# First feed-forward product of a hybrid decoder layer: high weights against both halves of an activation in one 512-column product, and the halves' sums by adding DMA

## The chip, the cores and the metric

The kernel runs on one core of one Trainium2 chip. The metric is device time in microseconds; lower is better. A core has TensorE (matrix products, "PE"; its weight loads are listed as "PEld"), VectorE ("DVE"), ScalarE ("ACT"), GpSimd ("POOL") and SyncE ("SP"). DMAs are issued from the queues of SP, ScalarE and GpSimd; those that add to their destination are issued from GpSimd's queue here.

## The reference

One decoder layer on 512 tokens and 2048 features, in float32. The change lies in the feed-forward part:

```
def conv_ffn(h, w_up, conv_w, conv_b, w_down):
    u, g = jnp.split(h @ w_up, 2, axis=-1)            # w_up: 2048 x 11264, u and g: 512 x 5632
    u = lax.conv_general_dilated(u, conv_w[:, None, :], ...) + conv_b   # causal, width 3, per channel
    return (jax.nn.silu(u) * g) @ w_down

...
h = rms_norm(x, norm_ffn[l]) * (1.0 + sc2) + sh2
x = x + g2 * conv_ffn(h, w_up[l], conv_w[l], conv_b[l], w_down[l])
```

Ahead of it stand a modulation (`c_act @ w_mod`), a combined input projection, two kinds of attention and an output projection; behind it `h @ w_down` and a last RMSNorm.

## The kernel before

**Precision by halves.** Every float32 factor is split into a high half (rounded to the float32r type by ScalarE) and a low half (the rest, by VectorE's subtraction); `split_to` (L214) and `cut` (L1028) do this. A product of two such factors is three matmuls: high weight by high activation, high weight by low activation, low weight by high activation.

**The first feed-forward product.** The 5632 channels are 44 tiles `f` of 128. The first three (`NP = 3`) are done plainly, each matmul 128 weights wide and 512 tokens long. The other 41 use a factored scheme with seven products instead of eight (Winograd's form of Strassen's): the 2048 features are halved, the 512 tokens are halved (`W = 256`), and the two outputs of a tile, u and g, are the halves of the third direction. `Duo` (L1109) is one of the seven products of a tile, in the order `ORDER = (1, 2, 6, 5, 7, 3, 4)`. Its `mm` runs 8 steps over the 128-feature pieces of a half, three matmuls of 256 columns per step, into one of three PSUM banks: x holds products 1, 6, 7 and 4, z holds 2, y holds 5 and 3. Products share a bank and go on adding to it, so between two products in one bank the running value is copied or added out (`Duo.out`, L1143): product 1's value and then product 6's out of x by a ScalarE copy (L1148, L1152), product 7's by a VectorE addition (L1157), and so on. The banks hold 512 columns; 256 are used.

**Operands.** `form[i]` holds the activation side of product i as (high, low) tiles. Forms 1, 2, 3 and 5 are blocks of the normed activations, kept in eight tiles `h2h0..3` and `h2l0..3` (L1596); forms 6, 7 and 4 are sums of blocks, made by `t_forms` (L1170); form 5 is written by `t1_form` (L1188) once the plain units have read what lay there. The weight side of a tile comes as four raw pieces of 128 x 1024 (512 KB), a and b for u, c and d for g. `duo_load` (L1067) fetches them through SP, `duo_cut` (L1078) makes the seven weight combinations: a is cut first, then b, then s = d - (a - c), then c + d, then a - c, b - s and d. A piece is fetched again for tile f + 2 once its last cut is made; even tiles lie in the pool `raw2`, odd ones in `fr`, so each piece has two buffers. A cut goes into one of four weight buffers, so cuts run up to three products ahead of TensorE.

**After the products.** In `out` for product 3 the kernel starts `conv` (L1035): ScalarE applies bias and one tap (L1036), VectorE the two other taps (L1037, L1038), ScalarE SiLU (L1039). For product 4, VectorE multiplies the first 256 columns by g straight out of bank x and the others by g in store (L1164, L1165), and ScalarE issues the store to DRAM.

**Order.** A program in the kernel writes down slots (one product each). `drive` (L374) issues the weight cuts of the slots up to three ahead, then a slot's matmuls, then one `step` of every generator that runs beside them (`start` adds one, with a delay in steps). What is written first has priority; a scheduler then gives each engine a fixed order of its instructions, in which one that it holds to be ready may go ahead of one written before it. On the chip each engine works its own list in that order. Beside the products, `mod_gen` (L260) works off the last modulation columns: GpSimd's queue loads 128 x 512 pieces (`raw_mod`, L1531, four buffers), VectorE multiplies and adds them (L231), 64 pieces in the stage, paced by the number of columns that TensorE was given.

Of the kernel before, what the change touches and what calls it, by code (L numbers as in the profile page):

```python
# [8 lines left out]
F32 = mybir.dt.float32  # L9
F32R = mybir.dt.float32r  # L10
AF = mybir.ActivationFunctionType
OP = mybir.AluOpType
# [3 lines left out]
P = 128  # L16
T = 512
# [16 lines left out]
def hybrid_trunk(ctx, tc, xT, cT, wm, bm, nrm, wik, wiq, wi1, sinks, kvn, wuk, wuv, rel, onehot,  # L34
# [4 lines left out]
    class Counted:  # L39

        def __init__(self, to):
            self.to, self.cols = to, 0
# [171 lines left out]
    def split_to(hi_t, lo_t, full, keep=False):  # L214
        hi = act.copy(hi_t, full)  # L215
        if keep:
            tc.keep_in_program_order(hi)
        dve.tensor_tensor(lo_t, full, hi_t.bitcast(F32), OP.subtract)  # L218
# [86 lines left out]
    def pace(gen, every):  # L305
        paced.append([gen, every, pe.cols])
# [650 lines left out]
    slots = []  # L957
# [47 lines left out]

    class Rows:

        def __init__(self, tiles):
            self.t = tiles

        def __getitem__(self, key):
            return self.t[key[1] // 4][:, :, key[1] % 4]

    acts, ugate = {}, {}
    x2d = [dram.tile([P, 4, T], F32, name=f"x2d{i}") for i in range(4)]
# [12 lines left out]
    def cut(x, name):  # L1028

        w = env["px0"].tile([P, 2, 1024], F32R, tag=f"x2_{cut_turn[0] % 4}", name=f"w{name}")  # L1030
        cut_turn[0] += 1
        split_to(w[:, 0], w[:, 1], x)
        return w[:, 0], w[:, 1]

    def conv(f, y, u):  # L1035
        act.activation(y, u, AF.Identity, bias=cb_sb[:, f:f + 1], scale=cw_sb[:, f, 2:3])  # L1036
        dve.scalar_tensor_tensor(y[:, 1:], u[:, :T - 1], cw_sb[:, f, 1:2], y[:, 1:], OP.mult, OP.add)  # L1037
        dve.scalar_tensor_tensor(y[:, 2:], u[:, :T - 2], cw_sb[:, f, 0:1], y[:, 2:], OP.mult, OP.add)  # L1038
        act.activation(y, y, AF.Silu)  # L1039
# [24 lines left out]

    duo_raw = {}

    def duo_load(f, tag):  # L1067
        if f >= FT:
            return
        row, half = {"a": (0, 0), "b": (0, 1), "c": (1, 0), "d": (1, 1)}[tag]  # L1070
        if f % 2:
            t = fr_tile(tag, f"r{tag}{f}")
        else:
            t = env["raw2"].tile([P, 1024], F32, tag=tag, name=f"r{tag}{f}")
        duo_raw[f, tag] = t
        sp.dma_start(t, wup[2 * f + row].rearrange("p a b -> p (a b)")[:, 1024 * half:1024 * half + 1024])

    def duo_cut(f, pos):  # L1078
        a, b, c, d = [duo_raw[f, t] for t in "abcd"]
        name = f"u{f}_{pos}"  # L1080
        if pos == 0:
            return cut(a, name)
        if pos == 1:
            w = cut(b, name)
            dve.tensor_tensor(a, a, c, OP.subtract)
            return w
        if pos == 2:
            s = duo_raw[f, "s"] = fr_tile("s", f"rs{f}")
            dve.tensor_tensor(s, d, a, OP.subtract)  # L1089
            return cut(s, name)  # L1090
        if pos == 3:
            dve.tensor_tensor(c, c, d, OP.add)
            w = cut(c, name)
            duo_load(f + 2, "c")
            return w
        if pos == 4:
            w = cut(a, name)
            duo_load(f + 2, "a")
            return w
        if pos == 5:  # L1100
            dve.tensor_tensor(b, b, duo_raw[f, "s"], OP.subtract)
            w = cut(b, name)
            duo_load(f + 2, "b")
            return w
        w = cut(d, name)
        duo_load(f + 2, "d")
        return w

    class Duo:  # L1109
# [11 lines left out]
        def mm(self, w):  # L1121
            box, i = self.box, ORDER[self.pos]
            if i == 1:
                box["x"] = bank("acc", f"ux{self.f}")[:, :W]
            elif i == 2:
                box["z"] = bank("sc", f"uz{self.f}")[:, :W]
            elif i == 5:
                box["y"] = bank("tp", f"uy{self.f}")[:, :W]
            ps = box[{2: "z", 5: "y", 3: "y"}.get(i, "x")]
            new = i in (1, 2, 5)  # L1130
            ah, al = form[i]
            go = {} if new else {"skip_group_check": True}
            for k in range(8):
                wh, wl = [x[:, P * k:P * k + P] for x in w]
                xh, xl = [x[k // 4][:, k % 4] for x in (ah, al)]
                pe.matmul(ps, wh, xh, start=new and k == 0, stop=False, **go)
                pe.matmul(ps, wh, xl, start=False, stop=False, **go)
                pe.matmul(ps, wl, xh, start=False, stop=k == 7, **go)

        def after(self):  # L1140
            start(self.out())
# [1 line left out]
        def out(self):  # L1143
            f, box, i = self.f, self.box, ORDER[self.pos]
            ut = env["ut"]
            if i == 1:
                box["u"] = ut.tile([P, T], F32, tag="u", bufs=2, name=f"ut{f}")
                act.copy(box["u"][:, :W], box["x"])  # L1148
            elif i == 2:
                dve.tensor_tensor(box["u"][:, :W], box["u"][:, :W], box["z"], OP.add)  # L1150
            elif i == 6:
                act.copy(box["u"][:, W:], box["x"])  # L1152
            elif i == 5:
                box["g"] = ut.tile([P, W], F32, tag="g", bufs=2, name=f"gt{f}")
                act.copy(box["g"], box["y"])
            elif i == 7:
                dve.tensor_tensor(box["g"], box["g"], box["x"], OP.add)  # L1157
            elif i == 3:
                dve.tensor_tensor(box["u"][:, W:], box["u"][:, W:], box["y"], OP.add)
                box["o"] = ut.tile([P, T], F32, tag="y", bufs=3, name=f"y{f}")  # L1160
                conv(f, box["o"], box["u"])
            else:
                y = box["o"]
                dve.tensor_tensor(y[:, :W], box["x"], y[:, :W], OP.mult)  # L1164
                dve.tensor_tensor(y[:, W:], box["g"], y[:, W:], OP.mult)  # L1165
                yield
                store_act(f, y)
            yield

    def t_forms():  # L1170

        x2, tt = env["x2"], env["tt"]
        h, l = [x.t for x in env["h2"]]
        for i, j, tok in ((1, 0, 0), (2, 2, 0), (3, 2, 1), (5, 0, 1)):
            form[i] = [[x[j + q][:, tok] for q in range(2)] for x in (h, l)]
        for i in (6, 7, 4):
            t = tt.tile([P, 2, 8, W], F32R, tag=f"t{i}", name=f"t{i}_up")
            form[i] = [[t[:, x, 4 * q:4 * q + 4] for q in range(2)] for x in range(2)]
        for j in range(2):
            q11, q12, q21, q22 = [x2[k][:, :, c:c + W] for k in (j, j + 2) for c in (0, W)]  # L1180
            for i, q, x, y, op in ((7, q22, q22, q12, OP.subtract), (None, q12, q12, q11, OP.subtract),
                                   (6, q11, q11, q22, OP.add), (4, q21, q21, q11, OP.subtract)):
                dve.tensor_tensor(q, x, y, op)
                if i:
                    split_to(form[i][0][j], form[i][1][j], q)
                    yield

    def t1_form():  # L1188
        for j in range(2):
            split_to(form[5][0][j], form[5][1][j], env["x2"][j][:, :, W:])  # L1190


    down_t = {}
# [335 lines left out]
        return two[0][:, kt % 2]  # L1529

    def raw_mod(g, kt):  # L1531
        t = env["ut"].tile([P, 512], F32, tag="mr", bufs=4, name=f"mraw{g}_{kt}")
        pool.dma_start(t, wm[g, kt // 4][:, kt % 4])  # L1533
        return t

# [57 lines left out]
    for dt in range(0, KT, 4):  # L1593
        dve.scalar_tensor_tensor(a2[:, dt:dt + 4], mod[:, 16 + dt // 4], 1.0, nrm_sb[:, 1, dt:dt + 4],
                                 OP.add, OP.mult)
    form_t = [[big.tile([P, 2, 4, W], F32R, tag=f"b{'hl'[i]}{j}", name=f"h2{'hl'[i]}{j}") for j in range(4)]  # L1596
              for i in range(2)]
    env["h2"] = [Rows(x) for x in form_t]
    halves = lambda x: x.rearrange("p (a b) -> p a b", a=2)
    for i in range(4):  # L1600
        for kt in range(4 * i, 4 * i + 4):
# [13 lines left out]
    ringc.__exit__(None, None, None)  # L1615
    rawc = tc.tile_pool(name="raw2", bufs=1, side="right", reuse_waits="tile")
    env["raw2"] = rawc.__enter__()
    for t in "abcd":
        duo_load(NP + 1, t)
    utc = tc.tile_pool(name="ut", bufs=1, side="right", reuse_waits="tile")  # L1620
    env["ut"] = utc.__enter__()
    pace(mod_gen(range(20, 24), raw_mod, 3, env["ut"], o_bank), 28000)
    drive(slots, marks["duo"], marks["down"] - 7, ahead=3)
    down_t["stage0"] = {}
    for k in range(2):
        for c in range(2):
            t = env["raw2"].tile([P, 1024], F32, tag="abcd"[2 * k + c], name=f"stage0_{k}{c}")
            down_t["stage0"][k, c] = t = t.rearrange("p (a b) -> p a b", a=4)
            sp.dma_start(t, actd[k][:, :, W * c:W * c + W])
    drive(slots, marks["down"] - 7, marks["down"] - 3, ahead=3)  # L1630
    down_tiles()
    for t in "acdb":
        for p in range(2):
# [122 lines left out]
```

## Time and profile before

| | before |
|---|---|
| median of 3 runs | 2130.55 us (2129.72 to 2136.72) |
| the profiled execution | 2132.93 us, of which its span is 2131.1 us |
| granted TensorE clock, mean | 0.994 |
| TensorE, VectorE, ScalarE, GpSimd busy | 98%, 81%, 54%, 8% of the span |
| stage of the factored products (827.8 to 1662 us) | 834.2 us, 6934 matmuls |

A profile's page lists busy time and shares of the span by engine. A grouped row has the line in the kernel, engine, operation, output <- inputs, shapes and count, then busy time, mean ns of one, and the idle time before them with what ended it. A row of the timeline has start, duration, engine, line, operation, tiles and count. Matmuls are pipelined, so the mean duration of one (283 ns for 256 columns) is longer than the distance from one to the next. Instructions on VectorE overlap a little too.

### The profile page before, as it was taken

The page shows a single profiled execution, that of the slowest core. Times are in us where ns is not written, and L with a number is a line of the kernel's source. Part 1 is how long each engine was busy: PE and PEld are TensorE (multiplying, and loading weights), DVE is VectorE, ACT ScalarE, POOL GpSimd, SP SyncE. Part 2 cuts the span into 40 slices and gives each one's busy share as a digit, 9 for nine tenths or more (in the row PEclk, how much of TensorE's full clock was granted, in tenths as well). Part 3 has the DMA queues.
Part 4 walks back from the last instruction along what each step waited for, and adds up shares of the span by engine and source line. Part 5 has one row for each costly group of instructions (what it writes and reads, how often), then busy time and mean ns, then how long its engine had stood idle before and what let it go on. Part 6 is the DMA issues. An engine that isn't in the chain of part 4 may idle for free.

```text
span 2131.1 us, 34497 instructions
## 1 busy us (share of the span) xinstructions
PE 2080.6 (98%) x13346; PEld 1832.2 (86%) x13346; DVE 1716.1 (81%) x2522; ACT 1143.2 (54%) x1907; POOL 180.4 (8%) x310
## 2 busy tenths in 40 slices
PE   8999999999999999999999999999999999999997
PEld 4777877777788889999999999999999787787787
DVE  2887899877868788888788888888887987787867
ACT  4324887777722274444444444444444575675654
POOL 0000000111033200000000000000000011111110
PEclk9999999999999999999999999999999999999998
DMA  9773122666699724444444435435344888898982
GB/s 390 272 289 111 55 72 60 186 212 215 192 374 319 241 83 141 157 134 134 148 116 158 140 118 159 137 126 159 122 132 126 282 248 216 228 235 209 217 232 83
DMA packets 125029, 385.18 MB, mean 181 GB/s; under 512 B 14783, under 2 KB 24015, under 8 KB 118080
## 3 DMA queue, kind: packets, MB, share of 16 engines
q1 hardware_dynamic: 84096, 257.16, 36.8%
q0 software_dynamic: 31264, 108.51, 19.3%
q10 hardware_dynamic: 9504, 17.31, 2.2%
q8 instruction: 104, 1.70, 0.3%
q14 instruction: 61, 0.50, 0.1%
HBM read 324.46 MB, written 58.46 MB: 180 GB/s over the span
## 4 chain that ended last, share of the span: by engine, by line
PE 80%; DVE 8%; DMA 5%; ACT 4%; issue 3%; POOL 0%; SPq 0%; DVEq 0%; POOLq 0%; ACTq 0%
PE ux L53 21%; PE p L53 14%; PE uy L53 11%; PE uz L53 5%; PE qip L53 4%; DMA qa<-in_wdn_dram 1%; DMA mraw<-in_wm_dram 1%; PE ckv L53 1%; PE mrow L53 1%; DVE wd L218 1%; PE o L53 1%; DVE wk L688 1%; DMA rawca<-in_wdn_dram 1%; DVE top L685 1%; PE mps L53 1%
## 5 line engine op out<-in xcount | busy, mean ns | idle before, releaser
L53 PE MATMUL p<-wd,af 128*128 128x512 f32 x1680 | 386.3, 391 | 12.4 <-DVE wd L218 9.6
L53 PEld LDWEIGHTS p<-wd,af 128*128 128x128 f32 x1680 | 315.5, 188 | 82.8 <-DVE wd L218 13.7
L53 PE MATMUL ux<-t_up,wu 128*128 128x256 f32 x2952 | 375.3, 283 | 0.0
L53 PEld LDWEIGHTS ux<-t_up,wu 128*128 128x128 f32 x2952 | 362.9, 192 | 0.9 <-DVE gt L1157 0.2
L53 PE MATMUL uy<-h2h,wu 128*128 128x256 f32 x1312 | 249.6, 283 | 0.0
L53 PEld LDWEIGHTS uy<-h2h,wu 128*128 128x128 f32 x1312 | 210.6, 192 | 0.0
L231 DVE SCALAR_TENSOR_TENSOR macc<-mraw,c_sb,macc 128x512 f32<-128x512 f32 x240 | 179.5, 748 | 9.8 <-DMA mraw<-in_wm_dram 7.8
L53 PE MATMUL uy<-h2l,wu 128*128 128x256 f32 x656 | 185.6, 283 | 0.0
L218 DVE TENSOR_TENSOR wu<-ra,wu 128x1024 fp32r<-128x1024 f32 x82 | 100.2, 1222 | 63.0 <-ACT wu L215 63.0
L215 ACT CAST wu<-rb 128x1024 fp32r<-128x1024 f32 x82 | 86.0, 1048 | 111.3 <-PE ux L53 63.3
L215 ACT CAST wu<-ra 128x1024 fp32r<-128x1024 f32 x82 | 85.7, 1045 | 100.6 <-PE uy L53 60.9
L53 PEld LDWEIGHTS uy<-h2l,wu 128*128 128x128 f32 x656 | 125.9, 192 | 0.0
L53 PE MATMUL uz<-h2h,wu 128*128 128x256 f32 x656 | 124.8, 283 | 0.0
L53 PE MATMUL ux<-h2h,wu 128*128 128x256 f32 x656 | 124.8, 283 | 0.0
L218 DVE TENSOR_TENSOR wu<-rb,wu 128x1024 fp32r<-128x1024 f32 x82 | 100.1, 1220 | 8.4 <-ACT wu L215 8.4
L53 PEld LDWEIGHTS ux<-h2h,wu 128*128 128x128 f32 x656 | 105.3, 192 | 0.0
L53 PEld LDWEIGHTS uz<-h2h,wu 128*128 128x128 f32 x656 | 105.3, 192 | 0.0
L1533 POOL DMA_DIRECT2D mraw<-in_wm_dram x64 | 34.3, 536 | 797.7 <-DVE macc L231 621.8
L218 DVE TENSOR_TENSOR wu<-rd,wu 128x1024 fp32r<-128x1024 f32 x41 | 50.2, 1225 | 63.8 <-ACT wu L215 63.8
L1344 ACT COPY ev<-p 128x512 f32<-128x512 f32 x140 | 81.5, 583 | 26.0 <-PE p L53 18.7
L215 ACT CAST wu<-rs 128x1024 fp32r<-128x1024 f32 x41 | 43.2, 1053 | 95.3 <-DVE rs L1089 53.3
L53 PE MATMUL ux<-h2l,wu 128*128 128x256 f32 x328 | 92.8, 283 | 0.0
(1739 smaller groups left out, 4792.9 us busy)
## 6 DMA issues: line engine op xcount, KB each, us to landing
mraw<-in_wm_dram POOLq DMA_DIRECT2D x160, 256.0 KB, 5.4
total<-ev POOLq DMA_DIRECT2D x70, 512.0 KB, 8.0
mraw<-in_wm_dram SPq DMA_DIRECT2D x32, 1024.0 KB
mraw<-in_wm_dram POOLq DMA_DIRECT2D x48, 512.0 KB, 6.6
ra<-in_wup_dram SPq DMA_DIRECT2D x41, 512.0 KB
rc<-in_wup_dram SPq DMA_DIRECT2D x41, 512.0 KB
rb<-in_wup_dram SPq DMA_DIRECT2D x41, 512.0 KB
rd<-in_wup_dram SPq DMA_DIRECT2D x41, 512.0 KB
```

The source lines that it names most:

```text
L53: return self.to.matmul(out, w, x, **kw)
L215: hi = act.copy(hi_t, full)
L218: dve.tensor_tensor(lo_t, full, hi_t.bitcast(F32), OP.subtract)
L231: tc.keep_in_program_order(dve.scalar_tensor_tensor(acc, t, cact[:, kt:kt + 1], acc, OP.mult, OP.add))
L685: dve.max(top[b][:, r], cur[b])
L688: dve.match_replace(wk[b], top[b][:, r], cur[b], -3e38)
L1344: act.copy(e[:, b], ps)
L1533: pool.dma_start(t, wm[g, kt // 4][:, kt % 4])
```

## The change

In the factored products:

- The step of three matmuls of 256 columns becomes two: the high weight meets high and low activation side by side, as one matmul of 512 columns, and the low weight meets the high activation in one of 256. The bank then holds two sums side by side, which have to be added: [:, 0] has high by high and low by high, [:, 1] has high by low.
- So the copies and additions out of PSUM are 512 columns wide (256 tokens, both sums). The two sums of u and of g's second half are added by a DMA on GpSimd's queue that adds one part of a tile to the other in SBUF; g's first half is copied by ScalarE and its second sum added by VectorE. `conv` starts two steps after product 4's output and reads the summed u; one multiply of 512 columns replaces two of 256.
- c + d is no longer made by VectorE for tiles past the first factored one: SP loads c a second time, into a tile e, and a DMA on GpSimd's queue adds d from DRAM to it. c has one buffer (in `fr`), and so has e (in `raw2`); both are fetched again one tile ahead instead of two.
- The normed activations lie in eight tiles of [high/low, token half, two pieces], so that both halves of a piece can be one operand; the forms change with them, and form 5 is made by four splits instead of two.
- Tiles: u is [2, 512] and g [3, 256] with two buffers each, y has two buffers instead of three, mod's raw pieces two instead of four (loaded one ahead instead of two). At the end of the stage the four first loads of the next stage go out one slot later, one of them into e's place.

```
 class Rows:
-    def __init__(self, tiles):
-        self.t = tiles
+    def __init__(self, tiles, part):
+        self.t, self.part = tiles, part
     def __getitem__(self, key):
-        return self.t[key[1] // 4][:, :, key[1] % 4]
+        return self.t[key[1] // 2][:, self.part, :, key[1] % 2]
...
+def duo_part(f, tag):
+    row, half = {"a": (0, 0), "b": (0, 1), "c": (1, 0), "d": (1, 1)}[tag]
+    return wup[2 * f + row].rearrange("p a b -> p (a b)")[:, 1024 * half:1024 * half + 1024]
+
+def duo_sum(f):
+    pool.dma_start(duo_raw[f, "e"], duo_part(f, "d"), accum_op=OP.add)
+    yield
+
 def duo_load(f, tag):
     if f >= FT:
         return
-    row, half = {"a": (0, 0), "b": (0, 1), "c": (1, 0), "d": (1, 1)}[tag]
-    if f % 2:
+    if f % 2 and tag != "e" or tag == "c":
         t = fr_tile(tag, f"r{tag}{f}")
     else:
         t = env["raw2"].tile([P, 1024], F32, tag=tag, name=f"r{tag}{f}")
     duo_raw[f, tag] = t
-    sp.dma_start(t, wup[2 * f + row].rearrange("p a b -> p (a b)")[:, 1024 * half:1024 * half + 1024])
+    sp.dma_start(t, duo_part(f, "c" if tag == "e" else tag))
+    if tag == "e":
+        start(duo_sum(f), 2)
...
     if pos == 1:
         w = cut(b, name)
         dve.tensor_tensor(a, a, c, OP.subtract)
+        if f > NP:
+            duo_load(f + 1, "c")
         return w
...
     if pos == 3:
-        dve.tensor_tensor(c, c, d, OP.add)
-        w = cut(c, name)
-        duo_load(f + 2, "c")
+        if f > NP:
+            w = cut(duo_raw[f, "e"], name)
+            duo_load(f + 1, "e")
+        else:
+            dve.tensor_tensor(c, c, d, OP.add)
+            w = cut(c, name)
+            duo_load(f + 1, "c")
         return w
...
 def mm(self, w):
-        box["x"] = bank("acc", f"ux{self.f}")[:, :W]
+        box["x"] = bank("acc", f"ux{self.f}", (P, 2, W))
...
-    ah, al = form[i]
...
         wh, wl = [x[:, P * k:P * k + P] for x in w]
-        xh, xl = [x[k // 4][:, k % 4] for x in (ah, al)]
-        pe.matmul(ps, wh, xh, start=new and k == 0, stop=False, **go)
-        pe.matmul(ps, wh, xl, start=False, stop=False, **go)
-        pe.matmul(ps, wl, xh, start=False, stop=k == 7, **go)
+        x = form[i][k]
+        pe.matmul(ps, wh, x, start=new and k == 0, stop=False, **go)
+        pe.matmul(ps[:, 0], wl, x[:, 0], start=False, stop=k == 7, **go)
...
 def out(self):
     if i == 1:
-        box["u"] = ut.tile([P, T], F32, tag="u", bufs=2, name=f"ut{f}")
-        act.copy(box["u"][:, :W], box["x"])
+        box["u"] = ut.tile([P, 2, T], F32, tag="u", bufs=2, name=f"ut{f}")
+        act.copy(box["u"][:, :, :W], box["x"])
     elif i == 2:
-        dve.tensor_tensor(box["u"][:, :W], box["u"][:, :W], box["z"], OP.add)
+        dve.tensor_tensor(box["u"][:, :, :W], box["u"][:, :, :W], box["z"], OP.add)
     elif i == 6:
-        act.copy(box["u"][:, W:], box["x"])
+        act.copy(box["u"][:, :, W:], box["x"])
     elif i == 5:
-        box["g"] = ut.tile([P, W], F32, tag="g", bufs=2, name=f"gt{f}")
-        act.copy(box["g"], box["y"])
+        box["g"] = ut.tile([P, 3, W], F32, tag="g", bufs=2, name=f"gt{f}")
+        act.copy(box["g"][:, 1:], box["y"])
     elif i == 7:
-        dve.tensor_tensor(box["g"], box["g"], box["x"], OP.add)
+        g = box["g"]
+        dve.tensor_tensor(g[:, 1:], g[:, 1:], box["x"], OP.add)
+        pool.dma_start(g[:, 1], g[:, 2], accum_op=OP.add)
     elif i == 3:
-        dve.tensor_tensor(box["u"][:, W:], box["u"][:, W:], box["y"], OP.add)
-        box["o"] = ut.tile([P, T], F32, tag="y", bufs=3, name=f"y{f}")
-        conv(f, box["o"], box["u"])
+        u = box["u"]
+        dve.tensor_tensor(u[:, :, W:], u[:, :, W:], box["y"], OP.add)
+        pool.dma_start(u[:, 0], u[:, 1], accum_op=OP.add)
     else:
-        y = box["o"]
-        dve.tensor_tensor(y[:, :W], box["x"], y[:, :W], OP.mult)
-        dve.tensor_tensor(y[:, W:], box["g"], y[:, W:], OP.mult)
+        g, x = box["g"], box["x"]
+        act.copy(g[:, 0], x[:, 0])
+        dve.tensor_tensor(g[:, 0], g[:, 0], x[:, 1], OP.add)
+        for _ in range(2):
+            yield
+        y = ut.tile([P, T], F32, tag="y", bufs=2, name=f"y{f}")
+        conv(f, y, box["u"][:, 0])
+        dve.tensor_tensor(y, y, g[:, 0:2].rearrange("p a b -> p (a b)"), OP.mult)
         yield
         store_act(f, y)
...
 def t1_form():
-    for j in range(2):
-        split_to(form[5][0][j], form[5][1][j], env["x2"][j][:, :, W:])
+    for q in range(4):
+        t = env["fq"][q]
+        split_to(t[:, 0, 1], t[:, 1, 1], env["x2"][q // 2][:, 2 * (q % 2):2 * (q % 2) + 2, W:])
...
-    t = env["ut"].tile([P, 512], F32, tag="mr", bufs=4, name=f"mraw{g}_{kt}")
+    t = env["ut"].tile([P, 512], F32, tag="mr", bufs=2, name=f"mraw{g}_{kt}")
...
-for t in "abcd":
+for t in "abde":
     duo_load(NP + 1, t)
...
-pace(mod_gen(range(20, 24), raw_mod, 3, env["ut"], o_bank), 28000)
-drive(slots, marks["duo"], marks["down"] - 7, ahead=3)
+pace(mod_gen(range(20, 24), raw_mod, 2, env["ut"], o_bank), 28000)
+drive(slots, marks["duo"], marks["down"] - 6, ahead=3)
```

More of the change, by code (lines that the diff above doesn't have):

```diff
@@ L1123, in mm @@
             if i == 1:
-                box["x"] = bank("acc", f"ux{self.f}")[:, :W]
+                box["x"] = bank("acc", f"ux{self.f}", (P, 2, W))
             elif i == 2:
-                box["z"] = bank("sc", f"uz{self.f}")[:, :W]
+                box["z"] = bank("sc", f"uz{self.f}", (P, 2, W))
             elif i == 5:
-                box["y"] = bank("tp", f"uy{self.f}")[:, :W]
+                box["y"] = bank("tp", f"uy{self.f}", (P, 2, W))
             ps = box[{2: "z", 5: "y", 3: "y"}.get(i, "x")]
             new = i in (1, 2, 5)
-            ah, al = form[i]
             go = {} if new else {"skip_group_check": True}
@@ L1172, in t_forms @@
         x2, tt = env["x2"], env["tt"]
-        h, l = [x.t for x in env["h2"]]
-        for i, j, tok in ((1, 0, 0), (2, 2, 0), (3, 2, 1), (5, 0, 1)):
-            form[i] = [[x[j + q][:, tok] for q in range(2)] for x in (h, l)]
+        for i, k0, tok in ((1, 0, 0), (2, 8, 0), (3, 8, 1), (5, 0, 1)):
+            form[i] = [env["fq"][(k0 + k) // 2][:, :, tok, k % 2] for k in range(8)]
+        made = {}
         for i in (6, 7, 4):
-            t = tt.tile([P, 2, 8, W], F32R, tag=f"t{i}", name=f"t{i}_up")
-            form[i] = [[t[:, x, 4 * q:4 * q + 4] for q in range(2)] for x in range(2)]
+            t = made[i] = tt.tile([P, 2, 8, W], F32R, tag=f"t{i}", name=f"t{i}_up")
+            form[i] = [t[:, :, k] for k in range(8)]
         for j in range(2):
@@ L1184, in t_forms @@
                 if i:
-                    split_to(form[i][0][j], form[i][1][j], q)
+                    split_to(*[made[i][:, x, 4 * j:4 * j + 4] for x in range(2)], q)
                     yield
     def t1_form():
-        for j in range(2):
-            split_to(form[5][0][j], form[5][1][j], env["x2"][j][:, :, W:])
+        for q in range(4):
+            t = env["fq"][q]
+            split_to(t[:, 0, 1], t[:, 1, 1], env["x2"][q // 2][:, 2 * (q % 2):2 * (q % 2) + 2, W:])
     down_t = {}
@@ L1595, in hybrid_trunk @@
                                  OP.add, OP.mult)
-    form_t = [[big.tile([P, 2, 4, W], F32R, tag=f"b{'hl'[i]}{j}", name=f"h2{'hl'[i]}{j}") for j in range(4)]
-              for i in range(2)]
-    env["h2"] = [Rows(x) for x in form_t]
+    env["fq"] = [big.tile([P, 2, 2, 2, W], F32R, tag=f"b{'hl'[q % 2]}{q // 2}", name=f"h2_{q}") for q in range(8)]
+    env["h2"] = [Rows(env["fq"], i) for i in range(2)]
     halves = lambda x: x.rearrange("p (a b) -> p a b", a=2)
@@ L1626, in hybrid_trunk @@
         for c in range(2):
-            t = env["raw2"].tile([P, 1024], F32, tag="abcd"[2 * k + c], name=f"stage0_{k}{c}")
+            t = env["raw2"].tile([P, 1024], F32, tag="abed"[2 * k + c], name=f"stage0_{k}{c}")
             down_t["stage0"][k, c] = t = t.rearrange("p (a b) -> p a b", a=4)
             sp.dma_start(t, actd[k][:, :, W * c:W * c + W])
-    drive(slots, marks["down"] - 7, marks["down"] - 3, ahead=3)
+    drive(slots, marks["down"] - 6, marks["down"] - 3, ahead=3)
     down_tiles()
```

## Prediction

> **What bounds the kernel now.** I read the page first, then the table of stretches for the stage that the change touches, then the order of instructions inside it, and last the landing times of DMAs. The page gives the shares of the span:
>
> ```profile
> span 2131.1 us, 34497 instructions
> ...
> PE 2080.6 (98%) x13346; PEld 1832.2 (86%) x13346; DVE 1716.1 (81%) x2522; ACT 1143.2 (54%) x1907; POOL 180.4 (8%) x310
> ```
>
> TensorE is busy for 98% of the span, so a change pays only if TensorE gets less to do, or costs if it is made to wait. The stretch from the first factored product to the last (827.8 to 1662 us) is even tighter:
>
> ```profile
> core 0: us, PE busy (x) PEld busy (x) DVE busy (x) ACT busy (x) POOL busy (x), PEclk, DMA share, GB/s
> 827.80:1662.00 834.20, 834.20 (x6934) 832.79 (x6933) 690.38 (x805) 388.43 (x495) 33.25 (x62) 1.00 0.45 143
> ```
>
> TensorE has no gap here and the granted clock is 1.00. VectorE fills 83% and ScalarE 47%, GpSimd (the queue that issues adding DMAs) 4%, the DMA engines 45%. There are 41 units of 7 products, 56 steps of three matmuls each, so 6888 of the 6934 matmuls are the subject of the change, and one unit takes 834.2/41 = 20.35 us (20.2 without the other 46 matmuls).
>
> **The products.** What counts is the spacing of matmuls, not the mean duration of one, since they overlap. First narrow ones (256 columns) of a factored product, then wide ones (512 columns) of the plain products just before the stage:
>
> ```profile
> 999.81 0.28 PE L53 MATMUL uy<-h2l,wu 128*128 128x256 f32 x1
> ...
> 1000.17 0.28 PE L53 MATMUL uy<-h2l,wu 128*128 128x256 f32 x1
> ...
> 1000.53 0.28 PE L53 MATMUL uy<-h2l,wu 128*128 128x256 f32 x1
> ```
>
> ```profile
> 790.11 0.39 PE L53 MATMUL g0ps<-h2l,g0r_3h 128*128 128x512 f32 x1
> ...
> 792.84 0.39 PE L53 MATMUL u1ps<-h2l,u1r_3h 128*128 128x512 f32 x1
> ```
>
> The h2l matmul comes back every 0.36 us with two others between, so a narrow one takes 120.0 ns. Between the two wide rows lie 12 spacings: 2.73/12 = 227.5 ns. A step is now 3 x 120.0 = 360.0 ns and becomes 227.5 + 120.0 = 347.5 ns. It saves 12.5 ns, 0.70 us per unit, and over 41 x 56 = 2296 steps **28.7 us**. A unit goes from 20.2 to 19.5 us, a product from 2.88 to 2.78 us. Weight loads fall from three to two per step; the narrow spacing already holds one load each, so nothing is added there. The wide plain products read an operand made of two strided halves too, so the form [2, 256] has a row.
>
> The Trainium skill speaks against this gain: "TensorE: Matmul & The Clock Gate", section "Back-to-back issue gap", gives N/2.4 + 2.5 ns, so 109 ns at 256 columns, and an estimate by it is 2.5 ns saved per step, 5.7 us in all. The trace differs (120.0 ns measured at a granted clock of 1.00), and I take the trace.
>
> **VectorE and ScalarE.** Rows of the grouped view, with shapes kept apart:
>
> ```profile
> L1092 DVE TENSOR_TENSOR rc<-rc,rd 128x1024 f32<-128x1024 f32 x41 | 50.0, 1219 | 0.0
> ...
> L543 DVE TENSOR_TENSOR qi<-qi,qip 128x512 f32<-128x512 f32 x56 | 38.3, 684 | 14.4 <-PE qip L53 13.7
> ...
> L1344 ACT COPY ev<-p 128x512 f32<-128x512 f32 x140 | 81.5, 583 | 26.0 <-PE p L53 18.7 <-DMA total<-ev 7.3
> ...
> L1036 ACT ACTIVATE y<-ut,cb_sb,cw_sb 128x512 f32<-128x512 f32 x41 | 33.4, 815 | 1.6 <-DVE ut L1159 1.6
> ...
> L1165 DVE TENSOR_TENSOR y<-gt,y 128x256 f32<-128x256 f32 x41 | 17.0, 416 | 0.0
> ...
> L1157 DVE TENSOR_TENSOR gt<-gt,ux 128x256 f32<-128x256 f32 x41 | 17.0, 414 | 0.2 <-PE ux L53 0.2
> ...
> L1152 ACT COPY ut<-ux 128x256 f32<-128x256 f32 x41 | 15.0, 366 | 0.0
> ```
>
> VectorE loses c + d (1.22 us, now an adding DMA). The three additions out of PSUM grow from 256 to 512 columns: 3 x (0.684 - 0.414) = 0.81 us. A fourth addition (0.41) is new, and two multiplies of 0.416 become one of at most 0.684. Sum: -1.22 + 0.81 + 0.41 - 0.15 = -0.15 us per unit. From 690.4/41 = 16.8 us it goes to 16.7, which is 86% of 19.5: still not the bound. ScalarE gains 3 x (0.583 - 0.366) + 0.37 = 1.0 us on 9.5, 54%. Both are hidden on the whole; the question is where a copy or addition out of PSUM gates the next product in the same bank.
>
> The order inside a unit shows how much room there is: VectorE's addition L1157, which must end before the next product into the same bank begins, then TensorE's and ScalarE's rows at the same places:
>
> ```profile
> 925.68 0.41 DVE L1157 TENSOR_TENSOR gt<-gt,ux 128x256 f32<-128x256 f32 x1
> ...
> 1005.35 1.22 DVE L218 TENSOR_TENSOR wu<-rb,wu 128x1024 fp32r<-128x1024 f32 x1
> 1006.48 0.41 DVE L1157 TENSOR_TENSOR gt<-gt,ux 128x256 f32<-128x256 f32 x1
> ...
> 1086.65 0.41 DVE L1157 TENSOR_TENSOR gt<-gt,ux 128x256 f32<-128x256 f32 x1
> ...
> 1089.92 0.41 DVE L1159 TENSOR_TENSOR ut<-ut,uy 128x256 f32<-128x256 f32 x1
> ```
>
> ```profile
> 1594.59 0.41 DVE L1157 TENSOR_TENSOR gt<-gt,ux 128x256 f32<-128x256 f32 x1
> ```
>
> ```profile
> 1006.77 0.28 PE L53 MATMUL uy<-h2h,wu 128*128 128x256 f32 x1
> 1006.95 0.74 PE L53 MATMUL ux<-t_up,wu 128*128 128x256 f32 x4
> ```
>
> ```profile
> 1088.73 3.04 PE L53 MATMUL ux<-t_up,wu 128*128 128x256 f32 x24
> 1097.37 3.04 PE L53 MATMUL ux<-t_up,wu 128*128 128x256 f32 x24
> ```
>
> ```profile
> 1094.75 1.05 ACT L215 CAST wu<-ra 128x1024 fp32r<-128x1024 f32 x1 [1.84 <-PE ux L53]
> 1095.70 0.63 ACT L1039 ACTIVATE y<-y 128x512 f32<-128x512 f32 x1
> 1096.23 0.35 ACT L1148 COPY ut<-ux 128x256 f32<-128x256 f32 x1
> ```
>
> At 1086.65 the addition ends 1.67 us before product 4 begins at 1088.73; most units look like this. At 1006.48 it stands behind a split of weights and ends 0.06 us before TensorE goes on, which is already 0.06 us late; so it goes in 8 of the 41 units (the first of them at 925.68, the last at 1594.59). There the longer addition (+0.27) and the shorter product before it (-0.10) both show: 8 x 0.37 = **3.0 us** lost. The copy at 1096.23 ends 0.79 us before product 6; with +0.22 and -0.10 some 0.47 us stay, so it costs nothing unless something is put ahead of it.
>
> **The adding DMAs.** Each unit gets three on GpSimd's queue: 512 KB into e from DRAM, 128 KB into g, 256 KB into u, and SP loads e besides (512 KB). Nothing in the trace adds from SBUF to SBUF, so I bound it by plain loads in this stage (256 KB) and the adding DMAs of the next stage (512 KB, to DRAM):
>
> ```profile
> L1533 POOL DMA_DIRECT2D mraw<-in_wm_dram x64: 536/536/538, 820.0 to 1561.3; - x64
> ...
> DMA to landing us min/median/max: 2.8/4.5/8.1
> ```
>
> ```profile
> L1291 POOL DMA_DIRECT2D total<-ev x62: 842/852/1181, 1692.9 to 2059.0; - x62
> ...
> DMA to landing us min/median/max: 5.3/8.4/17.0
> ```
>
> GpSimd's own work is at most 3 x 0.85 = 2.6 us of 19.5 on an engine that is 4% busy. The DMA engines move 143 GB/s at 45%, so 318 GB/s when full. A unit moves 2.9 MB now and would move 0.5 MB more by plain loads and 0.9 MB by addition; counted once that is 4.3 MB, 13.7 us or 70% of 19.5, and 85% if adding bytes count twice. It fits.
>
> For e the round is: cut (1.05 + 1.22), load, addition, next cut. With 4.5 and 8.4 us (the two medians) that is 15.2 of 19.5 us, so it is hidden at no cost; the worst landings (8.1 + 17.0) would make 27.4 and would not be. On GpSimd's queue e's addition waits for e's load, and behind it stand mod's loads, whose tiles fall from four to two; one multiply-add of mod comes about every 834.2/64 = 13 us, so a load of 8.1 us is still in time, cost nothing. g's sum is wanted last and costs nothing either.
>
> For u the addition lies on a path: L1159's sum, DMA, bias (L1036), taps, product, store. Before, L1036 followed L1159 directly. Nobody waits for the store, but ScalarE takes its instructions in order, so if the bias stands ahead of the cast and the copy out of bank x, a late DMA holds both. Counted from product 4's start (1088.73): the sum ends at 1.19 + 0.68 = 1.87, GpSimd starts the DMA at 1.92, it lands L later, then bias 0.8, cast 0.95 and copy 0.58, so the copy ends at 4.25 + L. Product 6 begins 3 x 2.78 = 8.34 after product 4. So there is no stall below **L = 4.1 us**, and L - 4.1 per unit above it. I put L for 256 KB near the plain loads (2.8 to 8.1, the same bytes and the same stage) and the bias behind the copy in at least half of the cases, since its priority is given out two steps later; so nothing in the forecast, 0 to 49 us (L = 5.3, the fastest landing of the larger adding DMAs) in the range.
>
> By the Trainium skill ("DMA: Bandwidth & Descriptors", "Anatomy of one DMA — SWDGE (gpsimd) path") a DMA takes about 2.0 us plus its bytes at 436 GB/s, an estimate of 2.6 us for u, which would never stall; the trace has 4.5 us as the median for those bytes, so I keep the risk.
>
> **The ends of the stage.** At the change to the second feed-forward product TensorE waits already:
>
> ```profile
> 1663.79 5.28 PE L53 MATMUL p<-wd,af 128*128 128x512 f32 x22 [1.03 <-DVE wd L218]
> 1671.67 3.77 PE L53 MATMUL p<-wd,af 128*128 128x512 f32 x15 [2.60 <-ACT af L215]
> ```
>
> The stage loads go out one product (2.8 us) later and VectorE has 0.8 us more to do near there; of these 0 to 3.6 us I take **1.5**. At the front the four smaller splits of form 5 replace two larger ones, hidden by the last plain unit.
>
> Sum against the profiled execution (2132.93 us, of which the span is 2131.1): 28.7 - 3.0 - 1.5 = 24.2 us saved, 2108.7. The median of the runs, 2130.55, lies 2.4 lower, so I forecast **2106 us**; with these terms' bounds 2097 (the full 28.7 and small stalls undone) to 2116.
>
> **Rivals.**
> - *ScalarE held by u's DMA.* For it: in-order issue, L's median of 4.5 just above 4.1, fuller DMA engines. Against: ScalarE idles 1.84 us ahead of the cast at 1094.75, and no 256 KB load need be slow while no weight load is in flight. Between L = 4.1 and 4.85 the loss (up to 31 us) eats the gain: 2106 to 2137. Above 4.85 the kernel is slower than before; at 5.3 us 41 x 1.2 = 49 us are lost: 2155 us.
> - *e's round becomes the period.* It decides once load and addition take over 17.2 us together (19.5 less 2.3), and is slower than now above 17.9; at 22 us the unit takes 24.3, 40 x 4.1 = 164 us slower, less what split weights in store hide. Only the worst landings speak for it.
> - *The wide product saves nothing.* Halves that lie apart could cost two narrow passes, 240 ns; then only the losses remain, 2130.55 + 4.5 = 2135. The plain products at 227.5 ns speak against it. The Trainium skill's formula cited above would give 2130.55 - 5.7 + 4.5 = 2129.
>
> **How the numbers follow.** A kernel like this one can be told from no change at about 0.3%, 6.4 us. Forecast 0.64; ScalarE held a little 0.12 (half of it still faster), held much 0.11; e's round 0.06; no saving from wide products 0.05; something else 0.02. Faster: 0.64 + 0.06 + 0.01 = 0.71; same: some 0.04 of the mild case, 0.05 and some of the rest, 0.12; slower: 0.17. The range goes from 2097 to 2138: it leaves out the heavy case and e's round.
>
> **What would show it.** Right: wide products at about 227 ns in alternation with narrow ones at 120, a unit of 19.5 us, a stage of about 804 us without gaps, VectorE at about 86%, DMA share 0.7 to 0.85. Wrong: TensorE idle before product 6 with ScalarE behind a DMA into ut; TensorE waiting for split weights with ScalarE waiting for e's addition; wide products at 240 ns.

## The result, and the profile after

The changed kernel takes 2117.19 us (median of 4 runs, 2116.02 to 2118.58) against 2130.14 us before; the ratio is 0.9934 with a 95% interval of 0.9912 to 0.9956. So it is faster by 13 us, about half of the 24 that I forecast. It lies inside the forecast range (2097 to 2138), but just above the 2116 that the bounds of the sum's own terms gave.

The page of the changed kernel, span and busy times:

```profile
span 2116.8 us, 30287 instructions
...
PE 2062.9 (97%) x11050; PEld 1708.6 (81%) x11050; DVE 1719.1 (81%) x2484; ACT 1184.1 (56%) x1950; POOL 287.0 (14%) x432
```

2296 matmuls have gone and GpSimd's share has grown from 8 to 14%. TensorE's share has fallen by one point although it has less to do: it now waits. The table of stretches for the factored products, from the first to the last:

```profile
core 0: us, PE busy (x) PEld busy (x) DVE busy (x) ACT busy (x) POOL busy (x), PEclk, DMA share, GB/s
827.90:1647.10 819.20, 813.47 (x4626) 705.17 (x4626) 689.62 (x761) 424.26 (x531) 139.00 (x183) 1.00 0.77 215
```

The stage lasts 819.1 us where it lasted 831.6 (from the first start to the last end of a product), at the same granted clock. VectorE is at 84% (forecast: about 86%), the DMA engines at 0.77 (0.7 to 0.85). The stage should have fallen to about 806 (831.6 less 28.7 plus 3.0), so 13 us are missing here. Two things show. First, the starts of products, in two places of the stage:

```profile
1003.00 2.99 PE L53 MATMUL ux<-t_up,wu 128*128 128x512 f32 x16
1005.83 3.00 PE L53 MATMUL ux<-h,wu 128*128 128x512 f32 x16
1008.66 2.98 PE L53 MATMUL uz<-h,wu 128*128 128x512 f32 x16
```

```profile
1054.43 2.94 PE L53 MATMUL uy<-h,wu 128*128 128x512 f32 x16
1057.20 2.94 PE L53 MATMUL ux<-t_up,wu 128*128 128x512 f32 x16
1059.98 2.94 PE L53 MATMUL uy<-h,wu 128*128 128x512 f32 x16
```

Products follow each other at 2.83 us in the first place and at 2.77 in the second, with no gap in either: 353 and 347 ns per step (one wide and one narrow matmul). Over all products the spacing keeps to one of the two for many products and then changes. 188 of 287 are slow ones. From the starts of all 4592 matmuls, a wide one takes 234.7 ns and a narrow one 116.3, a step 350.9 instead of 347.5.

Second, TensorE's waits. A row says which engine waited for whom, total, times and the longest:

```profile
PE ux L53 <- ACT ut L1161: 5.5, 7, 1.8
```

L1161 is ScalarE's copy of product 1 out of bank x, which product 6 waits for. These rows leave out short gaps and what the modelled ends hide; measured from start to start, the spacings beyond the normal ones add up to 10.0 us (1.7 before); some 8 of these microseconds lie ahead of product 6. The worst place, ScalarE's, TensorE's and GpSimd's rows:

```profile
1146.95 0.36 ACT L1179 COPY gt<-ux 128x256 f32<-128x256 f32 x1
1150.35 0.81 ACT L1036 ACTIVATE y<-ut,cb_sb,cw_sb 128x512 f32<-128x512 f32 x1 [3.04 <-issue]
1151.07 1.03 ACT L215 CAST wu<-ra 128x1024 fp32r<-128x1024 f32 x1
1152.00 0.57 ACT L1161 COPY ut<-ux 128x512 f32<-128x512 f32 x1
```

```profile
1147.94 2.94 PE L53 MATMUL uz<-h,wu 128*128 128x512 f32 x16
1152.63 1.54 PE L53 MATMUL ux<-t_up,wu 128*128 128x512 f32 x7 [1.75 <-ACT ut L1161]
```

```profile
1144.80 0.86 POOL L1176 DMA_DIRECT2D ut<-ut  x1 [0.89 <-DVE ut L1175]
```

u's adding DMA goes out at 1144.80 and the bias (L1036) starts at 1150.35. In between ScalarE does nothing for 3 us although the cast and the copy behind could run: product 1 had ended before 1148. The row calls this idle time "issue", so the profile names nothing that ended it. The landing does: the DMA lands at 1150.27, 5.47 us after its issue, and the bias starts 0.07 us later. Over all 41 units the bias starts 0.07 to 0.09 us behind this landing, but for one (0.35). The copy ends at 1152.57 and product 6 starts at 1152.63. In all 40 units the bias stands ahead of the copy of the next unit's product 1. How late u's DMA is (issue to landing, least, median, most):

```profile
L1176 POOL DMA_DIRECT2D ut<-ut x41: 842/857/880, 847.6 to 1655.2; - x41
...
DMA to landing us min/median/max: 3.2/3.5/5.5
```

The median of 3.5 is below the 4.1 us that I had worked out as the limit. But in 24 of 40 units VectorE makes the sum late (a multiply-add of mod stands two or five instructions ahead of it), and then GpSimd mostly issues 2.4 to 2.7 us after the end of product 3 instead of 1.9 to 2.0. So the median unit ends its copy only 0.4 us ahead of product 6, and in 11 units product 6 starts 0.15 to 1.9 us late. The two longest waits, of 1.9 and 1.7 us, come in the units with the two slowest landings of these 40 (5.47 and 5.07 us; why these two were slow isn't shown); in two others GpSimd issued 1.6 us after the end of the sum, and product 6 waited 1.2 and 0.3 us.

### The profile page after: what moved, and what is told of

It reads as the page before. It is cut to its first block, busy times and chain, and to the rows that moved or that the text cites. A ratio compares the mean times of both kernels' runs of the same rounds, so it can differ in the third digit from the quotient of the medians.

```text
span 2116.8 us, 30287 instructions
## 1 busy us (share of the span) xinstructions
PE 2062.9 (97%) x11050; PEld 1708.6 (81%) x11050; DVE 1719.1 (81%) x2484; ACT 1184.1 (56%) x1950; POOL 287.0 (14%) x432
## 4 chain that ended last, share of the span: by engine, by line
PE 78%; DVE 7%; DMA 6%; issue 4%; ACT 4%; POOL 0%; SPq 0%; DVEq 0%; POOLq 0%; ACTq 0%
PE ux L53 21%; PE p L53 14%; PE uy L53 10%; PE uz L53 5%; PE qip L53 4%; DMA qa<-in_wdn_dram 2%; DMA mraw<-in_wm_dram 2%; PE ckv L53 1%; PE mrow L53 1%; DMA rawca<-in_wdn_dram 1%; PE o L53 1%; DVE wk L688 1%; PE mps L53 1%; DVE wd L218 1%; DVE top L685 1%
## 5 line engine op out<-in xcount | busy, mean ns | idle before, releaser
L53 PE MATMUL p<-wd,af 128*128 128x512 f32 x1680 | 388.1, 393 | 11.5 <-DVE wd L218 11.5
L53 PE MATMUL ux<-t_up,wu 128*128 128x512 f32 (+1 forms) x1968 | 367.7, 339 | 5.7 <-ACT ut L1161 5.5
L53 PEld LDWEIGHTS ux<-t_up,wu 128*128 128x128 f32 x1968 | 300.6, 188 | 54.2 <-ACT ut L1161 10.0
L53 PE MATMUL uy<-h,wu 128*128 128x512 f32 (+1 forms) x1312 | 243.7, 338 | 0.0
L53 PEld LDWEIGHTS uy<-h,wu 128*128 128x128 f32 x1312 | 200.4, 188 | 29.8
L231 DVE SCALAR_TENSOR_TENSOR macc<-mraw,c_sb,macc 128x512 f32<-128x512 f32 x240 | 179.3, 747 | 10.1 <-DMA mraw<-in_wm_dram 8.3
L53 PE MATMUL ux<-h,wu 128*128 128x512 f32 (+1 forms) x656 | 123.9, 338 | 0.0
L53 PE MATMUL uz<-h,wu 128*128 128x512 f32 (+1 forms) x656 | 121.8, 338 | 0.0
L53 PEld LDWEIGHTS uz<-h,wu 128*128 128x128 f32 x656 | 100.2, 188 | 15.0
L53 PEld LDWEIGHTS ux<-h,wu 128*128 128x128 f32 x656 | 100.3, 188 | 14.8
L1312 POOL DMA_DIRECT2D total<-ev x62 | 52.9, 853 | 294.7 <-ACT ev L1365 229.6
L215 ACT CAST wu<-rd 128x1024 fp32r<-128x1024 f32 x41 | 43.1, 1052 | 46.5 <-PE ux L53 46.4
L218 DVE TENSOR_TENSOR wu<-rd,wu 128x1024 fp32r<-128x1024 f32 x41 | 50.2, 1224 | 20.7 <-ACT wu L215 20.3
```

Of the source, the lines that this page charges most:

```text
L53: return self.to.matmul(out, w, x, **kw)
L231: tc.keep_in_program_order(dve.scalar_tensor_tensor(acc, t, cact[:, kt:kt + 1], acc, OP.mult, OP.add))
L1312: tc.keep_in_program_order(pool.dma_start(to, x, accum_op=OP.add))
```

## The experiments

The first four ran on one chip, the next four on another, the last three on a third, each with runs of the kernel before beside them (medians 2130.61, 2131.82 and 2131.34 us). "Step" is the mean time of a step (a wide and a narrow matmul; three narrow ones in the kernel before and in most steps of `three_narrow`), "waits" the spacings beyond the normal ones, both from the starts of all matmuls of the stage in the profiled run. `grouped`, `bias_behind`, `three_narrow`, `c_plus_d_vector` and `vector_u_sum` are edits of the changed kernel; the later ones hold `bias_behind`'s edit as well.

| kernel | median us | ratio to before, 95% | stage us | step ns | waits us |
|---|---|---|---|---|---|
| before | | | 831.6 | 360.0 | 1.7 |
| changed | 2117.19 | 0.9934 (0.9912 to 0.9956) | 819.1 | 350.9 | 10.0 |
| grouped | 2119.78 | 0.9948 (0.9935 to 0.9961) | 817.4 | 349.1 | 12.2 |
| bias_behind | 2101.34 | 0.9862 (0.9849 to 0.9875) | 807.6 | 349.9 | 0.9 |
| three_narrow | 2135.14 | 1.0018 (1.0010 to 1.0027) | 833.3 | 359.0 | 5.6 |
| c_plus_d_vector | 2118.75 | 0.9939 (0.9926 to 0.9952) | 817.4 | 350.1 | 10.2 |
| vector_u_sum | 2105.46 | 0.9880 (0.9864 to 0.9897) | 805.0 | 348.7 | 1.0 |
| contiguous | 2105.10 | 0.9873 (0.9858 to 0.9888) | 806.7 | 349.4 | 0.9 |
| bias_behind_c_plus_d | 2104.10 | 0.9870 (0.9855 to 0.9884) | 807.6 | 349.8 | 0.9 |
| bias_behind_grouped | 2105.01 | 0.9873 (0.9859 to 0.9888) | 807.5 | 349.1 | 2.4 |
| strict_products | 2112.05 | 0.9910 (0.9894 to 0.9927) | 816.3 | 351.0 | 6.9 |
| vector_all | 2112.10 | 0.9910 (0.9897 to 0.9923) | 813.4 | 351.0 | 4.1 |
| bias_behind_again | 2105.84 | 0.9881 (0.9864 to 0.9898) | 805.8 | 349.0 | 1.0 |

**Is the slow rhythm one of alternating widths?** `grouped` puts a product's wide matmuls ahead of its narrow ones.

```
-for k in range(8):
-    ...wide k, narrow k
+for k in range(8):
+    pe.matmul(ps, w[0][:, P * k:P * k + P], form[i][k], start=new and k == 0, stop=False, **go)
+for k in range(8):
+    pe.matmul(ps[:, 0], w[1][:, P * k:P * k + P], form[i][k][:, 0], start=False, stop=k == 7, **go)
```

> Each product issues its eight wide matmuls first and its eight narrow ones behind them; same matmuls, same weight loads, everything else as in the changed kernel. Theory A (width alternation): in the changed kernel a wide and a narrow matmul in turn take 234.7 + 116.3 = 350.9 ns on average, some products 346.6 and others 353, where I had counted 227.5 + 120.0 = 347.5; this comes of the alternation, so here every wide one takes 227 and every narrow one 120, a product 2.78 us, the stage 7.8 us less than 819.1 and the time about 2109 us. Theory B (something else slows the reads, such as other engines or transfers): the mean over wide and narrow stays near 351 per step and the time near 2117 us. Both leave the waits for ScalarE's copy of product 1 (about 8 us) where they are.

The time does not fall. Grouped streams have two rhythms as well: wide ones at 226 to 228 ns in some products and at 231 to 236 in others. The mean step is 1.8 ns lower here, but with the waits away (`bias_behind_grouped`, below) grouping gains nothing either. Theory A is wrong: the slow rhythm comes without alternation too. Theory B as I had put it (other engines) is not shown by this.

**Does the bias hold ScalarE?** `bias_behind` queues the bias behind what is written before it.

```
 def conv(f, y, u):
-    act.activation(y, u, AF.Identity, bias=..., scale=...)
+    tc.keep_in_program_order(act.activation(y, u, AF.Identity, bias=..., scale=...))
```

> The bias step of the convolution is queued on ScalarE behind what is written before it, so it comes after the copy of product 1 instead of ahead of it; nothing else is changed. Theory A: in the changed kernel the bias waits for u's adding DMA at the head of ScalarE's queue and the copy behind it comes too late for product 6, which costs some 8 us in 9 units; here those waits vanish, the stage falls from 819 to about 811 us and the time to about 2109 us. Rival: the copy is late because ScalarE or VectorE has too much to do around a unit's end; then the waits stay, or turn up at product 7 behind the bias, and the time stays at about 2117 us.

The waits are gone. The table of stretches has no idle time of TensorE:

```profile
827.80:1635.50 807.70, 807.70 (x4626) 703.92 (x4626) 695.59 (x761) 425.83 (x532) 139.16 (x183) 1.00 0.79 218
```

ScalarE's rows in the same unit as above (the lines have moved by one: L1162 is the copy of product 1, L1037 the bias, L1166 the copy of product 6):

```profile
1144.91 0.36 ACT L1180 COPY gt<-ux 128x256 f32<-128x256 f32 x1
1146.16 1.05 ACT L215 CAST wu<-ra 128x1024 fp32r<-128x1024 f32 x1 [0.89 <-PE ux L53]
1147.12 0.58 ACT L1162 COPY ut<-ux 128x512 f32<-128x512 f32 x1
1148.92 1.05 ACT L215 CAST wu<-rb 128x1024 fp32r<-128x1024 f32 x1 [1.23 <-issue]
1149.88 0.81 ACT L1037 ACTIVATE y<-ut,cb_sb,cw_sb 128x512 f32<-128x512 f32 x1
```

```profile
1145.91 2.94 PE L53 MATMUL uz<-h,wu 128*128 128x512 f32 x16
1148.68 2.94 PE L53 MATMUL ux<-t_up,wu 128*128 128x512 f32 x16
```

The copy ends at 1147.70, a microsecond ahead of product 6 at 1148.68, and the bias comes when nobody waits. u's DMA lands as before (3.2, 3.5, 5.3 us): it isn't faster, only nobody stands behind it. The stage is 11.5 us shorter (9.1 of waits, 2.3 of steps). The kernel as a whole is 17 us shorter in the profile, so over 5 us lie outside the stage, where the two differ little in what they do. Over the kernels here the time outside the stage goes from 1292 (this one) to 1301 us, so these 5 us can't be put down to the edit. The same kernel ran once more on the third chip, to stand beside `strict_products` and `vector_all`:

> The kernel with the bias queued behind the copy once more, on the same chip as the two others of this call, to compare them with: 2101 to 2105 us. Which products fall into the rhythm of 353 ns may differ from the first run; the program is the same.

It takes 2105.84 us there (ratio 0.9881), with a stage of 805.8 us and 1.0 us of waits: the same to within the spread of the chips.

**The products alone.** `three_narrow` takes the wide product back from the second step of each product on (the first one starts both sums) and keeps everything else.

```
 for k in range(8):
-    pe.matmul(ps, wh, x, start=new and k == 0, stop=False, **go)
+    if k == 0:
+        pe.matmul(ps, wh, x, start=new, stop=False, **go)
+    else:
+        pe.matmul(ps[:, 0], wh, x[:, 0], start=False, stop=False, **go)
+        pe.matmul(ps[:, 1], wh, x[:, 1], start=False, stop=False, **go)
     pe.matmul(ps[:, 0], wl, x[:, 0], start=False, stop=k == 7, **go)
```

> The changed kernel with its wide product taken back: from the second step of each product on, high by high, high by low and low by high are three matmuls of 256 columns again, into the same two sums, while adding DMAs, tiles and outputs stay as changed. Theory A: a step takes 360 ns again instead of 350.9, for 2009 steps that is 18 us more; the longer products give u's DMA 0.2 us more room, so some 3 us of waiting go; the time is about 2132 us, a little over the kernel before. Rival (the gain is not the wide product's but comes from moving sums off VectorE): the time stays near 2117 us.

A step takes 359 ns and the kernel is 0.2% slower than before, close to what theory A gave. So the wide product is the whole gain, and the rest of the change costs about 4 us, with 5.6 us of waits in it.

**e's transfers.** `c_plus_d_vector` goes back to VectorE's addition for c + d; e's second load and its adding DMA go with it.

```
 if pos == 3:
-    if f > NP:
-        w = cut(duo_raw[f, "e"], name)
-        duo_load(f + 1, "e")
-    else:
-        ...
+    dve.tensor_tensor(c, c, d, OP.add)
+    w = cut(c, name)
+    duo_load(f + 1, "c")
```

> c + d is made by VectorE for every tile, as before the change; the second load of c and the adding DMA from DRAM are gone, the rest is as changed. Theory A: the DMA engines' share falls from 0.77 to about 0.57 and u's DMA lands nearer to its 3.2 us minimum, so most of the 8 us of waiting for the copy of product 1 goes; VectorE gets 1.13 us more per unit, 90% of the stage, still hidden: about 2110 us. Rival 1: e's transfers do not disturb u's; 2117 us. Rival 2: VectorE's extra work is what the adding DMA had been hiding; then products wait for split weights and the time is above 2120 us.

The DMA share falls and VectorE's rises as expected, but the wait stays:

```profile
829.10:1646.60 817.50, 811.39 (x4626) 705.00 (x4625) 729.20 (x801) 421.80 (x531) 104.93 (x143) 1.00 0.57 164
```

```profile
PE ux L53 <- ACT ut L1155: 6.1, 7, 1.8
```

u's DMA lands after 3.2, 3.3 and 5.1 us here: hardly sooner. Rival 1 holds: a DMA share of 0.77 is not what makes it late. With the waits gone the same holds:

> The bias queued behind the copy, and c + d made by VectorE for every tile, without e's load and adding DMA. Theory A: e's transfers cost nothing and VectorE's 1.13 us per unit are hidden (90% of a stage of 808 us), so the time is 2101 us within 3. Rival 1 (e's adding DMA is needed to keep VectorE ahead): products wait for split weights, above 2106 us. Rival 2 (the fuller DMA engines cost something at the ends of the stage): below 2098 us.

2104.1 us beside 2101 to 2106 for the kernel with e. e's second load and addition gain nothing that can be measured, and cost nothing.

**The DMA itself.** `vector_u_sum` leaves the bias ahead and lets VectorE add u's two sums.

```
-pool.dma_start(u[:, 0], u[:, 1], accum_op=OP.add)
+dve.tensor_tensor(u[:, 0], u[:, 0], u[:, 1], OP.add)
```

> The two sums of u are added by VectorE in SBUF instead of by a DMA; the bias stays ahead of the copy of product 1 in ScalarE's queue, as in the changed kernel. Theory A (the bias waits for u's DMA): the sum is there 3 us earlier, the waits for the copy of product 1 vanish, 0.6 us more per unit on VectorE stay hidden (88% of the stage), and the time is that of the kernel with the bias queued behind, about 2102 us. Rival (the place of the bias in the queue is what costs, whatever it waits for): the waits stay and the time is near 2117 us.

The waits vanish with the bias still in its place ahead of the copy. So it is neither the place nor the DMA alone, but an instruction that waits for a DMA at the head of a queue whose next copy TensorE needs.

**The two rhythms.** `contiguous` lays the halves side by side (with the tiles' shapes and their writers to match):

```
-return self.t[key[1] // 2][:, self.part, :, key[1] % 2]
+return self.t[key[1] // 2][:, key[1] % 2, :, self.part]
...
-form[i] = [env["fq"][(k0 + k) // 2][:, :, tok, k % 2] for k in range(8)]
+form[i] = [env["fq"][(k0 + k) // 2][:, k % 2, tok] for k in range(8)]
```

> The bias queued behind the copy, and the high and low halves of an operand side by side in SBUF, so that a wide matmul reads one run of 512 columns instead of two runs of 256 that lie 4 or 8 KB apart. The order of all instructions of TensorE is that of the kernel with the bias queued behind. Theory C (the slow rhythm, 353 instead of 347 ns per step, comes of the two runs): every step takes 347 ns, the stage falls from 807.6 to about 802 us and the time from 2101 to about 2096 us. Rival D (the rhythm is one that TensorE falls into by when a stream begins, whatever it reads): a mixture of 347 and 353 stays, 2101 us within 3.

> The bias queued behind the copy, and each product's eight wide matmuls ahead of its eight narrow ones. In the grouped run the products took 801.6 us where alternating ones took 805.6, and both had about 10 us of waits. If that difference is the order's, the stage falls to about 804 us and the time to 2097 us; if it was the chance of which rhythm a stream fell into, the time is 2101 us within 3.

Both mixtures stay: theory C is wrong, and the order of the matmuls isn't the cause either. Where does a stream change from one to the other? In the kernels with few waits it does so at mod's matmuls and at the ends of units, where the scheduler has put three matmuls of the next unit ahead of product 4 (rows of the changed kernel):

```profile
1142.38 0.75 PE L53 MATMUL ux<-h,wu 128*128 128x512 f32 x3
1142.97 2.94 PE L53 MATMUL ux<-t_up,wu 128*128 128x512 f32 x16
1145.74 2.36 PE L53 MATMUL ux<-h,wu 128*128 128x256 f32 x13
```

The changed kernel has this in 13 units. It is also why product 4 doesn't wait for VectorE's longer addition. `strict_products` forbids it:

```
+first = pe.matmul(ps, wh, x, start=new and k == 0, stop=False, **go)
+if k == 0:
+    tc.keep_in_program_order(first)
```

> The bias queued behind the copy, and each product's first matmul pinned behind all of the product written before it, so that no matmul of the next tile can go ahead of product 4. Theory A (the predicted loss before product 4 did not come because the next tile's first three matmuls were put ahead of it in about 13 units): the loss comes back, some 0.45 us in each of these units, 5 to 6 us in all, as waits of TensorE for VectorE's addition of product 7; about 2107 us beside 2101 to 2105 with the bias queued behind. If the rhythm of 347 or 353 ns per step changes only where the order is irregular or TensorE waits, it changes there and at mod's matmuls alone. Rival: the reordering hides nothing, and the time is that of the kernel with the bias queued behind.

```profile
PE ux L53 <- DVE gt L1174: 3.5, 11, 0.4
```

The wait before product 4 comes back in 11 units, some 0.48 us each from start to start (5.3 us), 6 us in the median beside `bias_behind_again`. In this kernel the rhythm changes at some of those waits and at some of mod's matmuls, and nowhere else; the longest stretch in one rhythm is over 60 products (1382 to 1562 us). So here a stream takes up one rhythm where it starts anew, and keeps it until it is interrupted. Why there are two, and what chooses, stays open. The kernel before has something like a start of this kind: TensorE begins at 763.15 behind a wait, and from 763.49 on eleven distances between its plain 512-column matmuls are 224 to 240 ns (mean 233, at a granted clock of 1.00) before they settle at 226 to 227. Whether that is the same thing isn't shown.

**Without adding DMAs.** `vector_all` gives c + d and the sums of u and of g's second half to VectorE, with the bias behind.

> The bias queued behind the copy, and no adding DMA in the stage: c + d, u's sum and g's sum are all VectorE's. Theory A (the adding DMAs do not shorten anything that TensorE waits for as long as VectorE keeps up, but all three together bring VectorE to its limit): VectorE gets 1.13 + 0.60 + 0.33 = 2.06 us more per unit, 780 of 808 us or 97% with the places where it waits for ScalarE not counted; products wait for split weights and the stage grows by 10 us or more: 2112 us or above. Rival (VectorE's lead of two products hides it all): 2101 to 2105 us, and the adding DMAs earn nothing.

```profile
828.00:1641.40 813.40, 813.40 (x4626) 705.94 (x4625) 764.12 (x881) 422.05 (x532) 33.26 (x62) 1.00 0.45 145
```

VectorE is at 94% and TensorE has no idle time to speak of; waits are 4.1 us instead of 1.0. The median is 2112 us, 6 more than that of `bias_behind_again` on the same chip. In the profiled runs the stage is 7.6 us longer, 3.1 of it waits and 4.6 the rhythm. The time is where theory A put its lower end, but the mechanism is only partly there: VectorE's lead hides most, and whether the rhythm's share has to do with the missing DMAs isn't shown. So the three adding DMAs together earn between 3 and 6 us, not ten.

## Why the prediction was right, and where it was off by half

- **The product, 28.7 us.** The mechanism was right (`three_narrow` shows that the gain is all here), the size was not. Products took 826.3 us before and 805.6 after: **20.7 us**. The step that failed is "becomes 227.5 + 120.0 = 347.5 ns": a step took 350.9 ns on average. I added spacings that I had read at one place each, from streams of one width, and had no row for the rhythm of 353 ns. The fast rhythm is 346.7, about as added up. `grouped` shows the slow one without alternation too, so mixing the widths is not shown to be its cause.
- **The Trainium skill's N/2.4 + 2.5 ns** ("TensorE: Matmul & The Clock Gate", "Back-to-back issue gap"), by which 5.7 us would have been saved, does not hold in this case: narrow matmuls came every 120.0 ns and plain wide ones every 227.5, and the products alone gave 20.7 us. There the Trainium skill gives this formula for the gap of an isolated matmul, a condition that the prediction left out.
- **3.0 us lost before product 4.** Did not come. The scheduler put three matmuls of the next tile ahead in 13 units (that it did so because the addition had grown is likely, but not shown); `strict_products` brings the loss back, 5.3 us in 11 units, so the mechanism was right and its size too small. I had taken the order of TensorE as fixed. The 8 units that I had counted start at 844.89, not at 925.68; the count stands.
- **ScalarE held by u's DMA, zero in the forecast.** The rival with 0.12 came, mildly: about **8 us**. The limit of L = 4.1 us was about right for a unit whose sum is on time. I had put L at 2.8 to 8.1 us and it was 3.2 to 5.5; but I left out that the sum itself is 0.6 to 0.7 us late in 24 of 40 units, and I gave the bias a place behind the copy "in at least half of the cases", where it stood ahead in all. Priority given two steps later did not help; why the scheduler chose this order isn't shown. This is the larger failure of judgement: the two bounds were there, and the forecast took the one without cost.
- **VectorE, ScalarE, DMA.** Right: 512-column additions took 0.68 us, copies 0.57 to 0.58, VectorE 84%, DMA share 0.77, GpSimd 139 us of 819.
- **e's round.** Hidden, as said: e's adding DMA lands after 5.7 to 10.1 us (median 8.5).
- **The ends, 1.5 us lost.** Outside the stage the span fell from 1299.5 to 1297.7 us, so 1.8 were gained. That is in the range in which these parts differ from kernel to kernel here (1292 to 1301 us).

Together: the products saved 20.7 us and the waits grew by 8.3 (from 1.7 to 10.0), which leaves 12.4 saved in the stage. With the 1.8 outside it the span is 14.3 us shorter (2131.1 to 2116.8) where 24.2 were forecast: 8.0 fewer from the products, 5.3 more lost in waits (8.3 instead of 3.0), and 3.3 better at the ends. So the forecast was right in its direction and its main mechanism. But a rival with a chance of 0.12 took about as much (8 us) as the products fell short by, and that the ends and the order before product 4 went the other way and gave some of it back is luck. With the bias behind the copy the kernel is 1.2 to 1.4% faster than before; with u's sum on VectorE instead (`vector_u_sum`) it is 1.2%, which can't be told from that.

## What to carry to other kernels

An adding DMA in place of an addition is cheap only as long as its reader isn't ahead of something urgent in an in-order queue: find the reader's place in the queue, and pin it behind. When a change lengthens one operation by 0.3 us, ask which margins are smaller than that, and whether the scheduler can still put other work there. A sum of spacings read from streams of one width gave about the best that the mixed stream reached here (347.5 against 346.7 ns), not its mean (350.9): read spacings at many places, and at the start of streams too.

## What the hardware showed that I had not expected

- TensorE alternating 512- and 256-column matmuls runs in one of two lasting rhythms, 346.7 or 353 ns per pair, at a granted clock of 1.00; the stream of 256-column matmuls before had one only (118 to 121 ns in all but 38 of 6883 distances, 120 in 6806). With all wide ones ahead of the narrow ones (`grouped`), or with the halves side by side (`contiguous`), a mixture of two stayed.
- An adding DMA of 256 KB within SBUF lands 3.2 to 5.5 us after its issue (median 3.5), in the median sooner than the plain loads of 256 KB from DRAM in the same stage (3.1 to 9.9, median 4.4); g's, half as large, took 2.8 to 8.2 (median 4.7):

```profile
L1172 POOL DMA_DIRECT2D gt<-gt x41: 842/855/879, 845.9 to 1642.8; - x41
...
DMA to landing us min/median/max: 2.8/4.7/8.2
```

- An adding DMA costs GpSimd 0.84 to 0.91 us to issue where a plain load takes 0.57 (median, same kernel), with VectorE 84% busy beside it.
